# Encoder block on one core: last LayerNorm's rows asked for on SP behind the last weights, joins at the fifth step, one rounding behind LayerNorm

## The chip, the cores and the metric

The kernel runs on one core of a Trainium2 chip. The metric is the device time of one execution in microseconds (us). Engines are named as in the profile: PE is TensorE, DVE VectorE, ACT ScalarE, POOL GpSimd, SP SyncE. SP issues most DMAs, POOL a few.

## The reference

One layer of a streaming encoder on 256 tokens of width 2048, in fp32. Each stage adds to the residual stream and ends in a LayerNorm:

```python
h = layer_norm(ALPHA * h + 0.5 * swiglu_ffn(h, ffn1_w_in[l], ffn1_w_out[l]), ln_ffn1_g[l], ln_ffn1_b[l])
mix = hybrid_mixer(h, w_in[l], gate_bias[l], ...)
h = layer_norm(ALPHA * h + mix, ln_mix_g[l], ln_mix_b[l])
xa = memory_cross_attention(h, mem, ...)
h = layer_norm(ALPHA * h + xa, ln_x_g[l], ln_x_b[l])
h = layer_norm(ALPHA * h + 0.5 * swiglu_ffn(h, ffn2_w_in[l], ffn2_w_out[l]), ln_ffn2_g[l], ln_ffn2_b[l])
```

`swiglu_ffn` is `(silu(x @ w_gate) * (x @ w_up)) @ w_out` with an inner width of 5504, that is 10 groups of 512 columns and one of 384. `layer_norm` ends with `* g + b`; the last one's g and b are rows of `t["gb"]`.

## The kernel before

Weights stream from memory in tiles of 128 x 2048 (1 MB; 128 x 1536 in the 384-column group) through three `raw` buffers. `fetch` (L181 to 186) has SP load one. `halves` (L245) splits it into two fp32r parts: ACT rounds the tile to `hi` (L250), DVE subtracts, `lo = raw - hi` (L253). TensorE multiplies hi by both halves of the activations and lo by the high half. There are two buffers each for `hi` and `lo` (`unit`); weights with named homes (X0, H5 and so on) are rounded into blocks of the activations' pool.

Some steps of a group are done as sums (`mm_sums`, L351): seven products in place of eight for a pair of weight tiles, for which DVE forms sums of the weights (L235, L237), ACT and DVE split those as well (`X` in the 384-column group's rows), and `shared` (L656 to L661) adds up four accumulators afterwards.

The order of work is a list of items. `run` (L172) walks it, and ahead of each item it builds the loads and the splitting of the next weights. Side items are put in by `weave` at given places of a list. A scheduler then orders each engine's instructions by priority and modelled readiness.

`ffn` (L536) runs the two FFNs. For each group of columns it makes the input products (`pair_group`: eight weight steps, of which 2, 4 and 6 are sums, and a `shared` item before the last), then `hidden` (L693): `product` forms silu(gate) * up (L705 to L708) and sorts the 16-bit words (L714), `send` has SP transpose them (L719), `turn` puts the words together again (ACT, L725) and splits them into hi and lo (ACT L242, DVE L243). This last step is called the join here. `send` and `turn` are woven into the next group, at its items 2 and 6; those of the last group, of 384 columns, into the out-projection. TensorE's rows of the 384-column group are L297 and L351 with 128x384; the out-projection follows at once with 128x512.

The last out-projection (`out_proj`, `skewed`) runs its last four weights first for one token half, then for the other, so that the first half's LayerNorm runs beside the second half's matmuls. `final_steps` (L1371) holds that LayerNorm. Its `load` fetches the rows g and b, each spread over the 128 partitions (1 MB each), into the blocks T0 and T1. DVE reads g at L1391 and b at L1395, POOL reads g at L1389.

`mixer` (L834) begins with the value projection `val`, also skewed: the four weights are used for token half 0 and then for token half 1, while the LayerNorm of the first FFN is turned into T (`ln_T`, L390). For each of four quarters `ln_T` normalizes (DVE L397 or ACT L399), transposes (TensorE L405), scales and shifts (ACT L412 and DVE L414 in turn) and splits into T (ACT L242, DVE L243). The third and fourth value weights have homes of their own; the fourth goes to X0 and X1.

Of the kernel before, what the change touches and what calls it, by code (L numbers as in the profile page):

```python
# [18 lines left out]
P = 128  # L19
S = 256  # L20
D = 2048
# [73 lines left out]
class Kernel:  # L95
# [76 lines left out]
    def run(self):  # L172
        queue = [w if isinstance(w, (tuple, Sums)) else (w, None) for _, ws, _, _ in self.items for w in ws]
        ready, nxt, live = [], 0, 0

        def slots(w):
            return 0 if isinstance(w, tuple) and w[1] else 1

        raws, sums = {}, {}

        def fetch(i):  # L181
            if i not in raws:
                ap = queue[i].ap if isinstance(queue[i], Sums) else queue[i][0]
                raws[i] = self.raw_tile()
                self.last_load = self.nc.sync.dma_start(raws[i][:, :ap.shape[1]], ap)
            return raws[i]

        def form_sums(i):
            if i < len(queue) and isinstance(queue[i], Sums) and i not in sums:
                raw, home = fetch(i), queue[i].stage  # L190
                sums[i] = self.weight_sums(raw, queue[i].m, self.block(home, (P, 2048)) if home else self.raw_tile())

        def load(i):
            w = queue[i]
            raw = fetch(i)
            form_sums(i)
            if isinstance(w, Sums):
                n = 4 * w.m
                got = self.halves(raw[:, w.m:n], *self.unit()), self.halves(
                    sums[i][:, :n], *(self.block(g, (P, 2048), F32R) for g in w.tags))  # L200
            else:
                ap, tags = w
                hi, lo = (self.block(g, (P, 2048), F32R) for g in tags[:2]) if tags else self.unit()
                got = self.halves(raw[:, :ap.shape[1]], hi, lo)
            form_sums(i + 1)
            return got

        def early(w):
            return not isinstance(w, Sums) and w[1] is not None and len(w[1]) > 2

        def ahead(need, held):
            if nxt < need:
                return True
            n = sum(not early(w) for w in queue[need:nxt])
            return (nxt < need + 5 and (early(queue[nxt]) or n < 2)
                    and held + live + slots(queue[nxt]) <= UNITS)

        done, highs = 0, []
        for fn, ws, held, prio in self.items:
            need = done + len(ws)  # L220
            while nxt < len(queue) and ahead(need, held):
                live += slots(queue[nxt])
                ready.append(load(nxt))
                highs.append(self.last_hi)
                nxt += 1
            got = [ready.pop(0) for _ in ws]
            live -= sum(slots(queue[done + i]) for i in range(len(ws)))
            done = need
            self.next_hi = highs[min(done, nxt - 1)] if highs else None
            with self.prio(prio):  # L230
                fn(*got)
# [7 lines left out]
        return t  # L239

    def split(self, src, hi, lo):
        self.nc.scalar.copy(hi, src)  # L242
        self.nc.vector.tensor_tensor(lo, src, hi.bitcast(F32), ALU.subtract)  # L243

    def halves(self, src, hi, lo):  # L245

# [143 lines left out]
    def ln_T(self, h, mr, tt, ln, xT, qs=range(4)):  # L390

        nc = self.nc
        mean, r, nb = mr
        for q in qs:
            hs = h[:, q * 512:(q + 1) * 512]
            if q % 2 == 0:
                nc.vector.tensor_scalar(hs, hs, mean, r, ALU.subtract, ALU.mult)  # L397
            else:
                nc.scalar.activation(hs, hs, AF.Identity, bias=nb, scale=r)  # L399
            ps = self.at_tile()  # L400

            with self.tc.issue_after(self.last_mm.ins):
                for j in range(4):
                    kt = 4 * q + j
                    nc.tensor.transpose(ps[:, j * P:(j + 1) * P], h[:, kt * P:(kt + 1) * P], self.ident)  # L405
            v = self.w2((P, 4, P))
            for j in range(4):
                kt = 4 * q + j
                g, b = self.vec(ln + "_g", kt), self.vec(ln + "_b", kt)
                src = ps[:, j * P:(j + 1) * P]  # L410
                if j % 2 == 0:
                    nc.scalar.activation(v[:, j, :], src, AF.Identity, bias=b, scale=g)  # L412
                else:
                    nc.vector.tensor_scalar(v[:, j, :], src, g, b, ALU.mult, ALU.add)  # L414
            hi, lo = (xT.blk(s, 4 * q, 4)[:, :, tt * P:(tt + 1) * P] for s in (0, 1))
            self.split(v, hi, lo)

    def ln_steps(self, ln, st, x):

# [116 lines left out]
    def ffn(self, tag, xT, st, first=None, steps=None, late=None, before=None, tags=None):  # L536
# [6 lines left out]
        for half, nf in enumerate(F_SPLIT):  # L543
            hid, fh, homes = Act([]), {}, SUMS_OUT[half]
            end = half == len(F_SPLIT) - 1
            form = lambda c, fh=fh, homes=homes, hid=hid: self.forms_step(fh, homes, c, lambda: hid)
            for g in range(-(-nf // 4)):
                j, n = f0 // 4 + g, min(4, nf - 4 * g)
                qs, ps = {}, {}
                if j == 2 and first is not None:  # L550
                    self.add(self.load_rest)
                if j == 0 and first is not None:
                    main, (ps, qs, fx) = [], first
                    self.add(lambda qs=qs: self.shared(qs, 512), prio=SOON)
                elif j == 0 and before:
                    main = self.collect(self.first_group, tag, xT, before, ps, fx)
                else:
                    src = t[tag + "_w_in"][j] if n == 4 else t[tag + "_w_in_r"][0]
                    main = self.collect(self.pair_group, bank, src, n * P, KT, xT, SUMS_IN, fx, ps, qs, None, SUM_HOME + ("H5",))
                self.weave(main, turn or {}, prio=0)  # L560
                for c, (home, _) in homes.items():
                    if home == "X1" and c // 2 == g - 1:
                        self.add(form(c))
                hidden, turn = self.hidden(ps, bank, g, n, hid, qs)
                self.add(hidden, prio=SOON)
                if before and 2 <= j < 6:
                    self.add(lambda q=j - 2: self.gb_apply(2, self.h, (q,)), prio=LATE)
                if j == 0 and first is not None:
                    for c in set(SUMS_IN) - set(AT_FIRST):
                        self.add(self.forms_step(fx, SUMS_IN, c, xT, False))  # L570
                bank ^= 1
            if end and late:
                self.add(late)
                self.add(lambda: setattr(self, "cut", True))

            def out(hid=hid):
                x = lambda: hid
                src = [t[tag + "_w_out"][g, :, f0 * 1024:(f0 + nf) * 1024] for g in range(2)]
                self.out_pair(bank, src[0], 0, nf, x, homes, fh, half == 0, st if end else None,
                              SUM_HOME + ("H5",) if end else SUM_HOME)  # L580
                if end:
                    self.out_proj(tag + "_w_out_r", nf, x, False, st, steps, tags, 2, cut=tags is None)
                else:
                    self.out_pair(bank ^ 1, src[1], 1, nf, x, homes, fh, half == 0, None)
            main = self.collect(out)

            side = dict(turn)
            for c, (home, k) in homes.items():
                if home == "X0":
                    side[4 + 2 * k] = side.get(4 + 2 * k, []) + [form(c)]  # L590
            if not end:
                for i in range(2):
                    side[len(main) - 3 + i] = [self.forms_step(fx, SUMS_IN, tuple(SUMS_IN)[i], xT)]
            self.weave(main, side, prio=0)
            turn = None
            f0 += nf
# [237 lines left out]
    def mixer(self, xT, st, steps):  # L834
# [7 lines left out]
        def val(n, tts, g, ps, tags=None, held=0, keep=False, again=False):  # L842
# [17 lines left out]
        ps = {}  # L860
        first = self.collect(lambda: self.skewed(
            lambda tt, g, **kw: val(0, (tt,), g, ps, **kw), (),
            (None, None, ("H5", "H0", "early"), ("X0", "X1"))))
        a, b, c = steps(1)
        self.weave(first, {0: a, 3: b, 4: c})
        gates, fx = {}, {}
# [504 lines left out]
    def final_steps(self, st):  # L1371
# [2 lines left out]

        def load():
            e["gb"] = [self.block(f"T{j}", (P, D)) for j in range(2)]
            for j in range(2):
                nc.gpsimd.dma_start(e["gb"][j], t["gb"][3, j:j + 1, :].to_broadcast([P, D]))

        def steps(tt):  # L1380
            def fn():
# [155 lines left out]
```

## Time and profile before

| what | value |
|---|---|
| median of 3 runs | 2466.49 us (2465.38 to 2469.66) |
| profiled execution | 2466.44 us |
| its span, first to last instruction | 2464.7 us |
| TensorE busy | 2445.8 us, 99% of the span |
| DVE, ACT busy | 2093.3 us (85%), 1447.0 us (59%) |
| DMA | 501.94 MB, mean 204 GB/s |
| mean granted TensorE clock | 0.998 |

Rows of a timeline are: start in us from the span's start, duration in us, engine, line, instruction, what it writes and reads, shape, count, and in brackets how long the engine was idle before it and whom it waited for. `x8` are eight instructions merged; the duration of merged matmuls reaches past the next row's start, since a matmul's end is modelled, so stretches are measured from start to start. SPq and POOLq are the queues of the engines that issue DMAs.

### The profile page before, as it was taken

What the parts mean: (1) busy time and instruction counts of PE and PEld (TensorE: products, weight loads), DVE (VectorE), ACT (ScalarE), POOL (GpSimd) and SP (SyncE); (2) the same over time, 40 slices, a digit from 0 to 9 for tenths busy, and PEclk for the clock granted to TensorE, in tenths of its full rate; (3) what the DMA queues carried; (4) which work ended last, traced back from release to release, by engine and by line L of the source; (5) the groups of instructions that cost most, each with busy time, mean ns of one, the idle gap of its engine ahead of it and who ended that gap; (6) DMA issues with size and microseconds to landing.
All of it is one profiled execution on the core that took longest, in us unless ns stands there. A gap on an engine that the chain in (4) does not pass through costs nothing.

```text
span 2464.7 us, 30068 instructions
## 1 busy us (share of the span) xinstructions
PE 2445.8 (99%) x11603; PEld 2048.8 (83%) x11603; DVE 2093.3 (85%) x2392; ACT 1447.0 (59%) x1932; POOL 37.6 (2%) x81
## 2 busy tenths in 40 slices
PE   9999999999999999999999999999999999999998
PEld 8888888888888888888888888888888888888876
DVE  8999989899778988688788798558879999888886
ACT  6676755676455556556455555545566675557562
POOL 0000000000000001000000000000000000000000
PEclk9999999999999999999999999999999999999999
DMA  7766656666645656554566557544556666666764
GB/s 265 253 217 215 211 203 203 215 197 223 244 156 200 211 205 227 178 174 140 176 235 220 188 179 239 190 161 154 188 197 207 229 221 207 220 213 202 232 210 140
DMA packets 118624, 501.94 MB, mean 204 GB/s; under 512 B 53936, under 2 KB 54704, under 8 KB 63312
## 3 DMA queue, kind: packets, MB, share of 16 engines
q1 hardware_dynamic: 112928, 479.96, 57.4%
q0 software_dynamic: 4688, 18.88, 2.4%
q8 instruction: 91, 1.49, 0.2%
q10 hardware_dynamic: 864, 1.18, 0.1%
q14 instruction: 53, 0.43, 0.1%
HBM read 485.30 MB, written 2.10 MB: 198 GB/s over the span
## 4 chain that ended last, share of the span: by engine, by line
PE 94%; DVE 3%; ACT 1%; DMA 1%; issue 1%; DVEq 0%; SPq 0%; ACTq 0%
PE at L297 24%; PE mm L297 24%; PE at L351 10%; PE mm L351 10%; PE mm L263 9%; PE mm L284 7%; PE mm L265 4%; PE at L986 1%; PE at L284 1%; DVE lo L253 1%; DMA raw<-ffn_w_in_r 1%; PE at L824 1%; PE at L1027 0%; PE at L1346 0%; ACT hi L250 0%
## 5 line engine op out<-in xcount | busy, mean ns | idle before, releaser
L250 ACT CAST hi<-raw 128x1024 fp32r<-128x1024 f32 (+1 forms) x852 | 804.8, 985 | 493.0 <-PE at L297 155.8
L253 DVE TENSOR_TENSOR lo<-raw,hi 128x2048 fp32r<-128x2048 f32 (+1 forms) x427 | 904.7, 2120 | 190.4 <-ACT hi L250 187.7
L297 PE MATMUL mm<-hi,T 128*128 128x512 f32 (+1 forms) x1232 | 288.8, 383 | 0.6 <-ACT hi L250 0.4
L250 ACT CAST X<-H 128x1024 fp32r<-128x1024 f32 (+1 forms) x166 | 170.7, 1034 | 171.3 <-DVE H L235 125.5
L297 PEld LDWEIGHTS mm<-hi,T 128*128 128x128 f32 x1232 | 229.0, 188 | 44.4 <-ACT hi L250 1.1
L297 PE MATMUL at<-hi,T 128*128 128x512 f32 x1072 | 256.7, 389 | 0.0
L253 DVE TENSOR_TENSOR X<-H,X 128x2048 fp32r<-128x2048 f32 (+1 forms) x83 | 186.7, 2250 | 65.0 <-ACT X L250 64.8
L297 PEld LDWEIGHTS at<-hi,T 128*128 128x128 f32 x1072 | 201.1, 188 | 42.0
L297 PE MATMUL mm<-lo,T 128*128 128x512 f32 (+1 forms) x616 | 148.2, 382 | 0.0
L297 PE MATMUL at<-hi,H 128*128 128x512 f32 x592 | 140.8, 390 | 0.0
L297 PE MATMUL at<-lo,T 128*128 128x512 f32 x536 | 132.5, 389 | 0.0
L297 PEld LDWEIGHTS mm<-lo,T 128*128 128x128 f32 x616 | 114.7, 188 | 20.9
L297 PEld LDWEIGHTS at<-hi,H 128*128 128x128 f32 x592 | 110.9, 188 | 23.5 <-DVE w L661 0.6
L263 PE MATMUL mm<-T,hi 128*128 128x512 f32 x512 | 123.7, 393 | 0.0
L297 PEld LDWEIGHTS at<-lo,T 128*128 128x128 f32 x536 | 100.6, 188 | 20.9
L237 DVE TENSOR_TENSOR H<-H,raw 128x512 f32<-128x512 f32 (+1 forms) x166 | 112.3, 676 | 2.3
L263 PEld LDWEIGHTS mm<-T,hi 128*128 128x128 f32 x512 | 93.8, 188 | 19.1 <-issue 0.7
L297 PE MATMUL mm<-hi,H 128*128 128x512 f32 x448 | 108.1, 391 | 0.0
L235 DVE TENSOR_TENSOR H<-raw 128x1024 f32<-128x1024 f32 (+1 forms) x83 | 99.4, 1198 | 4.5 <-DMA raw<-w_gate 4.4
L297 PEld LDWEIGHTS mm<-hi,H 128*128 128x128 f32 x448 | 83.6, 188 | 17.2 <-DVE w L272 0.2
L351 PE MATMUL mm<-X,X 128*128 128x512 f32 x348 | 93.1, 392 | 0.0
L250 ACT CAST X<-raw 128x1024 fp32r<-128x1024 f32 (+1 forms) x54 | 55.3, 1034 | 50.9 <-DVE raw L237 36.9
(331 smaller groups left out, 4074.1 us busy)
## 6 DMA issues: line engine op xcount, KB each, us to landing
raw<-ffn_w_in SPq DMA_DIRECT2D x150, 1024.0 KB, 4.9
raw<-ffn_w_out SPq DMA_DIRECT2D x66, 1024.0 KB, 4.9
raw<-w_gate SPq DMA_DIRECT2D x32, 1024.0 KB, 4.9
raw<-ffn_w_out_r SPq DMA_DIRECT2D x16, 1024.0 KB, 4.9
raw<-w_qk SPq DMA_DIRECT2D x16, 1024.0 KB, 5.0
raw<-w_o_b SPq DMA_DIRECT2D x16, 1024.0 KB, 4.8
raw<-w_out SPq DMA_DIRECT2D x16, 1024.0 KB, 4.9
raw<-w_xk SPq DMA_DIRECT2D x16, 1024.0 KB, 5.1
```

What stands on the lines that cost most here:

```text
L235: self.nc.vector.tensor_tensor(two[0], two[1], raw[:, :m].unsqueeze(1).to_broadcast([P, 2, m]), ALU.add)
L237: self.nc.vector.tensor_tensor(t[:, a * m:a * m + m], t[:, b * m:b * m + m], raw[:, a * m:a * m + m], ALU.add)
L250: self.last_hi = self.nc.scalar.copy(hi[:, c:d], src[:, c:d])
L253: self.nc.vector.tensor_tensor(lo[:, :n], src, hi[:, :n].bitcast(F32), ALU.subtract)
L263: self.nc.tensor.matmul(ps, hi[j], x.both(kt), start=(j == 0), stop=False)
L265: self.last_mm = self.nc.tensor.matmul(ps[:, :S], lo[j], x.at(0, kt), start=False, stop=(j == n - 1))
L284: self.last_mm = self.nc.tensor.matmul(ps, x.at(xi, kt)[:, tt * P:(tt + 1) * P], w[wi][:, j * 512 + c:j * 512 + c + m], start=(start and j ...
L297: self.last_mm = self.nc.tensor.matmul(ps[tt, g][:, :n], x.at(xi, kt)[:, tt * P:(tt + 1) * P], w[wi][:, c:c + n], start=first and j + wi + ...
L351: self.last_mm = self.nc.tensor.matmul(bank[:, :m], a[xi], v[wi][:, c * m:(c + 1) * m], start=own and first and wi + xi == 0, stop=own and ...
L824: self.nc.tensor.transpose(ps[:, i * P:(i + 1) * P], s[:, c:c + P], self.ident)
L986: nc.tensor.matmul(ps[:, c0:c0 + nk], q[:, tt * P:(tt + 1) * P], k[:, :nk], start=(j == 0), stop=(j == len(parts) - 1))
```

## The change

There are three edits.

First, `final_steps.load` issues the two row loads on SP instead of POOL, ordered behind the last weight load that has been built (`last_load`). Its item moves from ahead of the second FFN's last out-projection to six items before that projection's end, where all weight loads have been built.

Second, when the group is the one of 384 columns, the previous group's join is woven in at item 5 instead of 6, in both FFNs.

Third, the fourth value weight of the mixer gets the tag "turned", and its hi and lo are ordered, on ACT, behind the rounding of LayerNorm's second quarter (`ln_act`). The test for early weights looks for the tag's name in place of the number of tags, which finds the same weights as before.

```diff
@@ run / load
-                got = self.halves(raw[:, :ap.shape[1]], hi, lo)
+                with self.tc.issue_after(self.ln_act.ins) if tags and "turned" in tags else nullcontext():
+                    got = self.halves(raw[:, :ap.shape[1]], hi, lo)
@@ run / early
-            return not isinstance(w, Sums) and w[1] is not None and len(w[1]) > 2
+            return not isinstance(w, Sums) and w[1] is not None and "early" in w[1]
@@ split
-        self.nc.scalar.copy(hi, src)
+        copied = self.nc.scalar.copy(hi, src)
         self.nc.vector.tensor_tensor(lo, src, hi.bitcast(F32), ALU.subtract)
+        return copied
@@ ln_T
-            self.split(v, hi, lo)
+            turned = self.split(v, hi, lo)
+            if q == 1:
+                self.ln_act = turned
@@ ffn
+                if turn and n < 4:
+                    turn[5] = turn.pop(6)
                 self.weave(main, turn or {}, prio=0)
@@ ffn
             if end and late:
-                self.add(late)
                 self.add(lambda: setattr(self, "cut", True))
@@ ffn
             side = dict(turn)
+            if end and late:
+                side[len(main) - 6] = [late]
@@ mixer
-            (None, None, ("H5", "H0", "early"), ("X0", "X1"))))
+            (None, None, ("H5", "H0", "early"), ("X0", "X1", "turned"))))
@@ final_steps
-            for j in range(2):
-                nc.gpsimd.dma_start(e["gb"][j], t["gb"][3, j:j + 1, :].to_broadcast([P, D]))
+            with self.tc.issue_after(self.last_load.ins):
+                for j in range(2):
+                    nc.sync.dma_start(e["gb"][j], t["gb"][3, j:j + 1, :].to_broadcast([P, D]))
```

The line numbers of the changed kernel are higher by up to 8. On SP, at the end of the program, the order before was the last weights (`raw`) and then the output:

```order
L185 DMA raw_19153<-ffn_w_out_r 128x2048
L185 DMA raw_19160<-ffn_w_out_r 128x2048
L185 DMA raw_19179<-ffn_w_out_r 128x1536
L1396 DMA out<-h_101 128x512 x2
L1396 DMA out<-h_102 128x512 x2
```

Now the same place on SP holds the two rows of gb (T_2962 is the scale, T_2963 the offset), which POOL no longer issues:

```order
L185 DMA raw_19156<-ffn_w_out_r 128x2048
L185 DMA raw_19175<-ffn_w_out_r 128x1536
L1386 DMA T_2962_19206<-gb 128x2048
L1386 DMA T_2963_19207<-gb 128x2048
L1404 DMA out<-h_101 128x512 x2
```

They stand behind the last weight and ahead of the output.

On ACT, in the second half of the 384-column group of the first FFN, before the change (`hi_4294` is step 5's weight, `X_644` and `X_653` are the weight sums of steps 4 and 6, L725 and `H_658` the join, L656 and L657 are `shared`):

```order
L250 CAST hi_4294<-raw_4292 128x512
L250 CAST X_644_4263<-H_637_4227 128x1024
L250 CAST hi_4326<-raw_4299 128x1024
L250 CAST X_644_4263<-H_637_4227 128x512
L250 CAST hi_4326<-raw_4299 128x128
L250 CAST hi_4362<-raw_4360 128x1024
L250 CAST hi_4362<-raw_4360 128x512
L250 CAST X_653_4331<-H_650_4301 128x1024
L656 COPY w_662_4402<-at_4233 128x384
L250 CAST X_653_4331<-H_650_4301 128x512
L725 COPY w_614_4090<-w_615_4091 128x2x512
L725 COPY w_616_4092<-w_617_4093 128x2x512
```

And after the change, from the same cast on:

```order
L252 CAST hi_4294<-raw_4292 128x512
L732 COPY w_614_4090<-w_615_4091 128x2x512
L252 CAST X_644_4263<-H_637_4227 128x1024
L243 CAST H_655_4336<-w_614_4090 128x4x128
L252 CAST hi_4326<-raw_4299 128x1024
L252 CAST X_644_4263<-H_637_4227 128x512
L252 CAST hi_4326<-raw_4299 128x128
L732 COPY w_616_4092<-w_617_4093 128x2x512
L243 CAST H_655_4336<-w_616_4092 128x4x128
L252 CAST hi_4369<-raw_4367 128x1024
L252 CAST hi_4369<-raw_4367 128x512
L252 CAST X_653_4331<-H_650_4301 128x1024
```

One join now stands ahead of X_644's first cast and the other ahead of step 7's weight. On TensorE four matmuls of step 5 stand ahead of the first that reads X_644, where one stood. On DVE, at the end of the same group, the order before was (`lo_4398` is the low half of the first out-weight; L658 to L661 `shared`, L705 and L706 the product, and two rows of the join, L243):

```order
L243 TENSOR_TENSOR H_658_4367<-w_614_4090,H_658_4367 128x4x128
L658 TENSOR_TENSOR w_664_4404<-w_662_4402,at_4235 128x384
L243 TENSOR_TENSOR H_658_4367<-w_616_4092,H_658_4367 128x4x128
L659 TENSOR_TENSOR w_663_4403<-w_663_4403,w_664_4404 128x384
L706 TENSOR_TENSOR w_662_4402<-w_662_4402,mm_4156 128x384
L660 TENSOR_TENSOR w_664_4404<-w_664_4404,at_4236 128x384
L661 TENSOR_TENSOR w_665_4405<-w_663_4403,at_4236 128x384
L706 TENSOR_TENSOR w_664_4404<-w_664_4404,mm_4158 128x384
L705 TENSOR_TENSOR w_663_4403<-w_663_4403,mm_4157 128x384
L705 TENSOR_TENSOR w_665_4405<-w_665_4405,mm_4159 128x384
L253 TENSOR_TENSOR lo_4398<-raw_4395,hi_4397 128x2048
```

Now it is:

```order
L255 TENSOR_TENSOR lo_4398<-raw_4395,hi_4397 128x2048
L665 TENSOR_TENSOR w_664_4404<-w_662_4402,at_4235 128x384
L666 TENSOR_TENSOR w_663_4403<-w_663_4403,w_664_4404 128x384
L713 TENSOR_TENSOR w_662_4402<-w_662_4402,mm_4156 128x384
L667 TENSOR_TENSOR w_664_4404<-w_664_4404,at_4236 128x384
L668 TENSOR_TENSOR w_665_4405<-w_663_4403,at_4236 128x384
```

The low half moved ahead of all these, and the join's subtractions to earlier in the group. The second FFN has the same rows under other numbers.

On ACT, where the mixer starts, before (`X_786` is the fourth value weight; L412 with `w_773` to `w_779` are the pieces of LayerNorm's quarters 0 to 3; `T_768` and `T_769` the first two quarters' roundings):

```order
L399 ACTIVATE h_101<-h_101,nb_5094,y_5091 128x512 x2
L250 CAST X_786_5226<-raw_5224 128x1024
L412 ACTIVATE w_773_5151<-at_5146,vecs 128x128
L250 CAST X_786_5226<-raw_5224 128x1024
L412 ACTIVATE w_773_5151<-at_5146,vecs 128x128
L412 ACTIVATE w_775_5164<-at_5159,vecs 128x128
L242 CAST T_768_5141<-w_773_5151 128x4x128
```

After the change:

```order
L401 ACTIVATE h_101<-h_101,nb_5094,y_5091 128x512 x2
L414 ACTIVATE w_773_5151<-at_5146,vecs 128x128
L414 ACTIVATE w_775_5164<-at_5159,vecs 128x128
L414 ACTIVATE w_773_5151<-at_5146,vecs 128x128
L414 ACTIVATE w_775_5164<-at_5159,vecs 128x128
L243 CAST T_768_5141<-w_773_5151 128x4x128
L243 CAST T_769_5142<-w_775_5164 128x4x128
L252 CAST X_786_5226<-raw_5224 128x1024
```

Both casts of X_786 stand behind the two roundings now.

## Prediction

> **What bounds the kernel now.** I read the page first (engines, then the chain that ended last), then TensorE's waits, then the timelines of the engines around each wait.
>
> ```profile
> PE 2445.8 (99%) x11603; PEld 2048.8 (83%) x11603; DVE 2093.3 (85%) x2392; ACT 1447.0 (59%) x1932; POOL 37.6 (2%) x81
> ...
> PE 94%; DVE 3%; ACT 1%; DMA 1%; issue 1%; DVEq 0%; SPq 0%; ACTq 0%
> ```
>
> TensorE (PE) works 2445.8 of 2464.7 us and holds 94% of the chain. The edits change none of its matmuls, so only its stalls can be won. Its waits name them:
>
> ```profile
> PE at L351 <- ACT X L250: 2.1, 3, 1.0
> PE at L297 <- DVE lo L253: 2.0, 2, 1.0
> ...
> PE mm L284 <- DVE T L243: 0.4, 1, 0.4
> PE mm L284 <- ACT T L242: 0.3, 1, 0.3
> ```
>
> The columns are the total, the count and the longest in us. The first row lies in the 384-column group of the second FFN, the second behind that group in both FFNs, and the last two where the mixer starts. These are the three places of the change.
>
> **Part one: scale and offset behind the last weights.** The 384-column group runs twice with the same instructions, once per FFN, but only in the second do the two gb loads fall into it. TensorE's timeline (start, duration, instruction, count, idle before):
>
> ```profile
> 547.79 2.96 PE L297 MATMUL mm<-hi,T 128*128 128x384 f32 x16
> ...
> 551.98 2.93 PE L297 MATMUL mm<-hi,T 128*128 128x384 f32 x16
> ...
> 565.62 0.34 PE L297 MATMUL mm<-hi,T 128*128 128x384 f32 x1
> ...
> 572.38 0.51 PE L351 MATMUL mm<-hi,T 128*128 128x384 f32 x2
> ...
> 580.44 3.97 PE L297 MATMUL at<-hi,H 128*128 128x512 f32 x16
> 585.43 2.11 PE L297 MATMUL at<-lo,H 128*128 128x512 f32 x8 [1.03 <-DVE lo L253]
> ```
>
> ```profile
> 2313.69 2.96 PE L297 MATMUL mm<-hi,T 128*128 128x384 f32 x16
> ...
> 2349.55 4.02 PE L297 MATMUL at<-hi,H 128*128 128x512 f32 x16
> 2354.57 2.11 PE L297 MATMUL at<-lo,H 128*128 128x512 f32 x8 [0.99 <-DVE lo L253]
> 2356.51 3.79 PE L297 MATMUL at<-hi,H 128*128 128x512 f32 x16
> 2360.14 1.98 PE L297 MATMUL at<-lo,H 128*128 128x512 f32 x8
> ```
>
> From the group's first matmul to the same low-half matmul the first FFN takes 585.43 - 547.79 = 37.64 us, the second 2354.57 - 2313.69 = 40.88. The **3.24 us** between them are what the loads cost, if they are the cause. The DMA issues in the two stretches (550 to 575, then 2316 to 2343), with the median time to landing:
>
> ```profile
> raw<-ffn_w_in_r SPq DMA_DIRECT2D x4, 768.0 KB, 4.5
> ```
>
> ```profile
> raw<-ffn_w_in_r SPq DMA_DIRECT2D x4, 768.0 KB, 6.4
> T<-gb POOLq DMA_DIRECT2D x2, 1024.0 KB, 6.7
> ```
>
> The same four weight tiles take 1.9 us longer each beside the two gb loads, and the chain there runs through them. Moved away, they leave the first FFN's timing: I take 3.24; the bounds are 0 (the weights are late for another cause) and 3.24.
>
> Where they go, behind the last weight on SP, must be free too. The last weight's issue, its landing, and who reads it and the two rows:
>
> ```profile
> 2430.43 0.33 SPq L185 DMA_DIRECT2D raw<-ffn_w_out_r  x1
> ```
>
> ```profile
> raw<-ffn_w_out_r SPq DMA_DIRECT2D x1, 768.0 KB, 4.2
> ```
>
> ```profile
> 2436.20 3.95 DVE L253 TENSOR_TENSOR X<-raw,X 128x2048 fp32r<-128x2048 f32 x2
> ...
> 2444.24 0.74 DVE L1391 SCALAR_TENSOR_TENSOR h<-h,mv,T 128x512 f32<-128x512 f32 x1
> ...
> 2448.63 2.73 DVE L1395 SCALAR_TENSOR_TENSOR h<-h,y,T 128x512 f32<-128x512 f32 x4
> ```
>
> The scale would be issued near 2430.8. If it lands one 6.7 behind the weight's own landing at 2434.6, that is 2441.3, 2.9 us before L1391 reads it; the offset another 6.7 later, 2448.0, still before L1395. These are contended times, one after the other, so a pessimistic case. SP's later work, the output's DMAs, waits for L1395 in any case. I cost the new place at nothing. The trace has no broadcast on SP; the nearest row for a slow one is
>
> ```profile
> X<-gate_row POOLq DMA_DIRECT2D x4, 512.0 KB, 6.2
> ```
>
> and at its rate 1 MB takes 12.4 us: that is the upper bound, used in the last rival.
>
> **Part two: joins one step earlier.** Sixteen full-width matmuls normally take 2360.14 - 2356.51 = 3.63 us before the low half starts. Behind the 384-column group it is 585.43 - 580.44 = 4.99 and 2354.57 - 2349.55 = 5.02: 1.36 + 1.39 = **2.75 us** lost, waiting for VectorE's low half of the first out-weights, which stands behind the joins' two subtractions, the sums and the hidden product:
>
> ```profile
> 582.17 1.01 DVE L705 TENSOR_TENSOR w<-w,mm 128x384 f32<-128x384 f32 x2
> 583.10 2.28 DVE L253 TENSOR_TENSOR lo<-raw,hi 128x2048 fp32r<-128x2048 f32 x1
> ```
>
> In the changed order ten operations of VectorE no longer stand ahead of that low half: two subtractions of the joins, four of the sums, four of the product. At 0.5 each (the first row has two in 1.01) it starts near 578.1 and ends near 580.4, and TensorE asks for it at 580.44 + 3.63 = 584.07. What becomes late instead: the sums (L660, L661) free the fourth accumulator up to 2.28 us later, and the changed order puts that accumulator's matmuls last. So I count the 2.75 whole.
>
> The price is paid in step 5. There ScalarE now makes one join copy before it rounds the sums' weights X:
>
> ```profile
> 538.91 1.35 ACT L725 COPY w<-w 128x1024 uint16<-128x1024 uint16 x1
> ...
> 562.87 1.57 ACT L250 CAST hi<-raw 128x1024 fp32r<-128x1024 f32 x2 [3.17 <-PE mm L297]
> ```
>
> The casts end at 564.44, the copy at 565.79, and X's first cast (about 1.05) at 566.84. TensorE now has four matmuls ahead of it instead of one, at (551.98 - 547.79) / 24 = 0.175 us each, so it comes at 565.62 + 0.70 = 566.32 and **waits 0.5**. But this step already loses as much: its 36 matmuls should take 6.30 us and take 572.38 - 565.62 = 6.76. After X's first part the changed order has work enough for the rest of X. I take the net at 0; the bounds per group are +0.46 (old wait gone, none new) and -2 (a whole join, 1.35 and about 0.6 of rounding, shows). The second join fits into ScalarE's idle time before step 7.
>
> On SP one out-weight load now goes ahead of the two transposes of the 384-column hidden block. Those are read by
>
> ```profile
> 608.80 2.00 ACT L725 COPY w<-w 128x768 uint16<-128x768 uint16 x2
> ```
>
> more than 20 us after the out steps begin at 580.44: nothing.
>
> **Part three: one rounding behind LayerNorm.** The mixer's first matmuls need LayerNorm's first two quarters; on ScalarE two casts of the fourth value weight (X, which TensorE reads only in the fourth value step) stand between their pieces. ScalarE's, TensorE's and VectorE's rows:
>
> ```profile
> 697.09 1.14 ACT L242 CAST T<-w 128x512 fp32r<-128x512 f32 x2
> ```
>
> ```profile
> 681.22 1.04 PE L405 MATMUL at<-ident,h 128*128 128x128 f32 x8
> ...
> 684.18 1.04 PE L405 MATMUL at<-ident,h 128*128 128x128 f32 x8
> 685.55 0.50 PE L284 MATMUL mm<-hi,T 128*128 128x512 f32 x1 [0.34 <-ACT T L242]
> ...
> 689.10 2.00 PE L284 MATMUL mm<-hi,T 128*128 128x512 f32 x8
> ...
> 694.58 1.04 PE L405 MATMUL at<-ident,h 128*128 128x128 f32 x8
> 695.37 2.98 PE L284 MATMUL mm<-X,T 128*128 128x512 f32 x12
> ```
>
> ```profile
> 697.74 1.29 DVE L243 TENSOR_TENSOR T<-w,T 128x512 fp32r<-128x512 f32 x2 [0.25 <-ACT T L242]
> ```
>
> Eight transposes take 695.37 - 694.58 = 0.79, so the twelve matmuls could run from 684.97 and need 12 x 0.227 = 2.72, to 687.69. They end at 689.10: **1.41 us** lost. The second token half shows the chain without casts between: transposes at 694.58, T rounded by 697.66 (+3.1), low half by 698.4 (+3.8). From the first half's transposes at 681.22 that gives 684.3 and 685.0: just in time. Behind the casts that now wait stand the third and fourth quarters' pieces, some 2 us later; TensorE reads those two steps of 2.72 after 684.97, at 690.4. VectorE's low half of X keeps its place behind the second half's scaling. That half's own chain then has little room, for which I take off 0.15: 1.25, between 0 and 1.41.
>
> **Sum.** 3.24 + 2.75 + 0 + 1.25 = 7.24. The profiled execution took 2466.44 us (span 2464.7 and 1.74 around it); the median of the runs is 2466.49, so one number serves for both: 2466.44 - 7.24 = **2459.2**.
>
> **The rivals.**
> - *The joins' wait only moves.* ScalarE, first in first out, shows a join before X in each group. At the bound of -2 twice, less the 2.75, part two is -1.25 and the time 2463.2; half of it gives 2461.2. For it: X is just in time already. Against: four matmuls moved ahead of it.
> - *The weights of the second group are late for another cause.* Then part one is worth nothing and the time is 2462.4. Against: 4.5 against 6.4 in the two landing rows.
> - *The last weight is slowed by the row loads behind it.* If it lands like the contended ones (6.4, not 4.2), VectorE's last low half moves from 2440.15 to 2442.35. TensorE asks for it 18 matmuls after the row below starts, at 2441.5: 0.8 lost, 2460.0. For it: on another queue these loads did slow the weights. Against: here they are issued only behind the weight.
>
> ```profile
> 2437.45 4.93 PE L284 MATMUL mm<-X,H 128*128 128x512 f32 x21
> ```
>
> The Trainium skill (DMA: Bandwidth & Descriptors, "Two DMAs through the same engine are not ordered") says that descriptors of one queue start in order, but that a later one may finish before an earlier one has written. By that the weight could be late as in this rival, and by plain order in the queue it would land in 4.2 as before; no run here shows it yet.
> - *The rows land late: slower.* At gate_row's rate, one after the other behind the weight, the offset lands at 2434.6 + 24.8 = 2459.4, 10.8 after L1395 wants it; 10.8 - 7.24 gives 2470.0. It costs from a landing after 2448.6, and the kernel is slower than before once that is 7.2 later. Against: the gb rows took 6.7 each with weights beside them, on the other queue.
>
> **How the numbers follow.** Forecast 0.62 (own range 2457.8 to 2461.5), joins 0.16, other cause 0.08, last weight 0.08, late rows 0.04, anything else 0.02. The low end, 2457.4, is every bound at its best (3.24 + 2.75 + 0.92 + 1.41 = 8.3, and a little for the scatter of runs); the high end, 2463.6, takes in the first two rivals. Within 0.2% (about what a measurement of this kernel can tell from no change) means above 2461.6. Faster 0.71, same 0.24, slower 0.05.
>
> **What would show it.** In the new profile the two low-half waits behind the 384-column groups are gone; the second group's weights land in 4.5 again and it takes as long as the first; TensorE runs through the mixer's first twelve matmuls in under 3 us; a new wait of about half a us for X stands in step 5 of both groups. The forecast is wrong if X's wait is over 1 us, if L1391 or L1395 waits for a DMA, or if the stalls come back as waits further on.

## The result and the profile after

| kernel | median, us | runs | ratio to the kernel before |
|---|---|---|---|
| before | 2467.88 (2465.38 to 2469.66) | 7 | |
| after | 2458.82 (2458.64 to 2460.78) | 7 | 0.9967 [0.9957, 0.9977] |

The change gains 0.33%, 8.1 us by the ratio. The forecast was 2459.2, a gain of 7.24. The first profiled execution of the changed kernel is the slowest of its seven, 2460.78 us with a span of 2459.0; a second one, told below, has 2457.5. The page of the first, engines and then chain:

```profile
PE 2443.1 (99%) x11603; PEld 2048.7 (83%) x11603; DVE 2093.3 (85%) x2392; ACT 1447.9 (59%) x1932; POOL 36.6 (1%) x79
...
PE 98%; DVE 1%; ACT 0%; issue 0%; DMA 0%; DVEq 0%; SPq 0%; ACTq 0%
```

TensorE runs the same 11603 matmuls; its share of the chain rose from 94% to 98%, because waits went. TensorE's waits in that execution (total, count, longest):

```profile
PE at L407 <- issue: 1.9, 1, 1.9
PE at L479 <- DVE w L456: 1.1, 1, 1.1
PE at L353 <- ACT X L252: 0.4, 2, 0.2
```

The waits for X (2.1 in three) and for the low half (2.0 in two) of before are gone, but for two of 0.2. The second row stood before too, at the kernel's start. The first row, 1.9 at the transposes of LayerNorm, is new ("issue" means that the profile shows nothing that was waited for); the experiments come to it. TensorE's timelines of the two 384-column groups, first FFN, then second:

```profile
565.40 0.86 PE L299 MATMUL mm<-hi,T 128*128 128x384 f32 x4
566.44 0.98 PE L353 MATMUL at<-X,X 128*128 128x384 f32 x4 [0.19 <-ACT X L252]
...
580.17 2.92 PE L299 MATMUL at<-hi,H 128*128 128x512 f32 x12
...
585.65 3.79 PE L299 MATMUL at<-hi,H 128*128 128x512 f32 x16
```

```profile
2312.80 2.96 PE L299 MATMUL mm<-hi,T 128*128 128x384 f32 x16
...
2331.68 0.97 PE L353 MATMUL at<-X,X 128*128 128x384 f32 x4 [0.19 <-ACT X L252]
...
2345.39 2.92 PE L299 MATMUL at<-hi,H 128*128 128x512 f32 x12
...
2350.87 3.79 PE L299 MATMUL at<-hi,H 128*128 128x512 f32 x16
```

The second group's out step starts 2345.39 - 2312.80 = 32.59 us after the group, 35.86 before; the step lasts 2350.87 - 2345.39 = 5.48 with no wait in it, 6.96 before. The low half that TensorE used to wait for, on VectorE, and the weights of the second group (issues from 2312 to 2340, median time to landing last):

```profile
578.17 2.28 DVE L255 TENSOR_TENSOR lo<-raw,hi 128x2048 fp32r<-128x2048 f32 x1
```

```profile
raw<-ffn_w_in_r SPq DMA_DIRECT2D x5, 768.0 KB, 4.3
```

It starts at 578.17 where 583.10 was, and the weights land in 4.3, where 6.4 were, with no gb beside them. The rows and the last weight at their new place (issues from 2420 to 2440; SP's timeline; VectorE's readers):

```profile
T<-gb SPq DMA_DIRECT2D x2, 1024.0 KB, 7.8
...
raw<-ffn_w_out_r SPq DMA_DIRECT2D x1, 768.0 KB, 4.7
```

```profile
2425.16 0.90 SPq L1386 DMA_DIRECT2D T<-gb  x2
```

```profile
2438.74 0.74 DVE L1399 SCALAR_TENSOR_TENSOR h<-h,mv,T 128x512 f32<-128x512 f32 x1
...
2443.13 2.73 DVE L1403 SCALAR_TENSOR_TENSOR h<-h,y,T 128x512 f32<-128x512 f32 x4
```

The two rows land 6.8 and 8.8 us behind their issues (7.8 is the median of the two), by 2434.4 at the latest, and are read from 2438.7 and 2443.1 on: both readers carry no bracket, so nothing waits.

All that follows is read at three places. From the first matmul of each 384-column group: to the start of the out step, and to that of the next step behind it (24 matmuls on). At the mixer: from the transposes of LayerNorm's third and fourth quarters to the end of the first twelve matmuls. In us, from TensorE's timelines of one profile each:

| kernel | first FFN's group | second FFN's group | mixer | span |
|---|---|---|---|---|
| before | 32.65 / 39.59 | 35.86 / 42.82 | 4.92 | 2464.7 |
| after | 32.60 / 38.08 | 32.59 / 38.07 | 3.81 | 2459.0 |
| e1_rows | 32.60 / 39.55 | 32.37 / 39.36 | 5.27 | 2461.6 |
| e2_joins | 32.64 / 38.12 | 36.02 / 41.50 | 4.37 | 2461.5 |
| e3_round | 32.62 / 39.58 | 35.24 / 42.19 | 3.66 | 2462.7 |
| e4_rows_sp_old | 32.48 / 39.42 | 33.10 / 40.54 | 5.29 | 2464.6 |
| e5_rows_pool_late | 32.42 / 39.39 | 36.15 / 43.10 | 4.44 | 2464.3 |
| e6_joins4 | 32.51 / 37.99 | 32.63 / 38.11 | 3.63 | 2457.1 |
| e7_after_again | 32.62 / 38.10 | 32.61 / 38.09 | 3.60 | 2457.5 |
| e8_join_behind_x | 32.44 / 37.92 | 32.43 / 37.91 | 3.63 | 2457.1 |
| e9_after_sp_old | 32.65 / 38.14 | 33.69 / 39.17 | 3.62 | 2458.5 |
| e10_one_row | 32.64 / 38.12 | 33.96 / 39.44 | 3.80 | 2459.0 |
| e11_after_pool_old | 32.70 / 38.18 | 34.14 / 39.62 | 3.67 | 2461.1 |

### The profile page after: what moved, and what is told of

It reads as the page before. It is cut to its first block, busy times and chain, and to the rows that moved or that the text cites. A ratio compares the mean times of both kernels' runs of the same rounds, so it can differ in the third digit from the quotient of the medians.

```text
span 2459.0 us, 30064 instructions
## 1 busy us (share of the span) xinstructions
PE 2443.1 (99%) x11603; PEld 2048.7 (83%) x11603; DVE 2093.3 (85%) x2392; ACT 1447.9 (59%) x1932; POOL 36.6 (1%) x79
## 3 DMA queue, kind: packets, MB, share of 16 engines
q8 instruction: 91, 1.49, 0.2%
## 4 chain that ended last, share of the span: by engine, by line
PE 98%; DVE 1%; ACT 0%; issue 0%; DMA 0%; DVEq 0%; SPq 0%; ACTq 0%
PE mm L299 25%; PE at L299 25%; PE at L353 11%; PE mm L353 11%; PE mm L286 9%; PE mm L265 9%; PE mm L267 4%; PE at L993 1%; PE at L286 1%; PE at L831 1%; PE at L1034 0%; PE at L1353 0%; PE at L1329 0%; PE at L407 0%; DVE h L1403 0%; PE at L1035 0%
```

## The experiments

### Each part alone

The theory is the prediction's: three stalls, each undone by its own edit. The rivals are that the joins' wait only moves, and that the second group is late for another reason.

**e1_rows**: the kernel before, with the first edit only.

```diff
-                self.add(late)
+                side[len(main) - 6] = [late]
...
-                nc.gpsimd.dma_start(e["gb"][j], t["gb"][3, j:j + 1, :].to_broadcast([P, D]))
+            with self.tc.issue_after(self.last_load.ins):
...
+                    nc.sync.dma_start(e["gb"][j], t["gb"][3, j:j + 1, :].to_broadcast([P, D]))
```

> Only the two row loads are moved (SP, behind the last weight); joins and the mixer's rounding stay as before. Theory (the loads took bandwidth from the second 384-column group's weights): the second group takes 37.6 us from its first matmul to the first low half of the out-projection, like the first group (before 40.9), the four 768 KB weights land in 4.3 to 5.0 us (before 6.4), the low-half wait of 1.0 us behind both groups stays, and the time falls by 3.2 us. Rival one (those weights are late for another cause): the group stays at 40.9 and the time within 1 us. Rival two (the last weight or the rows come late at the end): the last weight lands over 6 us after its issue, or VectorE waits for a DMA in the last LayerNorm, and part of the 3.2 is lost there.

Measured 2463.47 us (2462.73 to 2466.74) against 2466.9, ratio 0.9988 [0.9980, 0.9997]. TensorE's second group:

```profile
2314.15 2.96 PE L297 MATMUL mm<-hi,T 128*128 128x384 f32 x16
...
2346.52 3.98 PE L297 MATMUL at<-hi,H 128*128 128x512 f32 x16
2351.53 2.14 PE L297 MATMUL at<-lo,H 128*128 128x512 f32 x8 [1.03 <-DVE lo L253]
2353.51 3.80 PE L297 MATMUL at<-hi,H 128*128 128x512 f32 x16
```

It falls to the first's times, 39.36 against 39.55, and the low-half wait stays in both. The rows beside its weights were the cause of all the 3.2 us between the groups.

**e2_joins**: the kernel before, with the second edit only.

```diff
+                if turn and n < 4:
+                    turn[5] = turn.pop(6)
```

> Only the joins are moved to the fifth step of the 384-column group. Theory (VectorE's queue ahead of the out-projection's first low half cost TensorE 1.4 to 1.5 us in each FFN): from the group's first matmul to the second out step the first FFN takes 38.1 us (before 39.6), the low-half waits are gone, a wait of 0.2 us for X stands in step 5, and the time falls by 2.9 us; the second group keeps the 3.2 us of the row loads. Rival (the wait only moves): X's wait in step 5 is 1 us or more per group, or the low-half wait is still there, and the time stays within 1 us.

Measured 2462.9 us (2460.23 to 2466.04), ratio 0.9984 [0.9975, 0.9993]. Both out steps are 5.48 long: the low-half waits go without the rows' help. In the first group the join's price in step 5 is a wait of 0.20 and the group's time to the out step is as before (32.64). In the second, still beside the rows, TensorE waits 1.69 for X.

**e3_round**: the kernel before, with the third edit only.

```diff
+                with self.tc.issue_after(self.ln_act.ins) if tags and "turned" in tags else nullcontext():
```

> Only the fourth value weight's rounding is ordered behind LayerNorm's second quarter. Theory (two casts in ScalarE's queue held back the first quarters): from the transposes of quarters 2 and 3 to the end of the mixer's first twelve matmuls 3.8 us (before 4.9), later steps as before, the time falls by 1.1 us. Rival (the chain from statistics to transposes sets it, not the casts): it stays at 4.9, or the 1.1 us come back as waits for the third quarter or for X within the next 20 us; the time stays within 0.3 us.

Measured 2465.7 us (2462.61 to 2467.7), ratio 0.9991 [0.9982, 0.9999]. TensorE at the mixer:

```profile
684.21 1.04 PE L407 MATMUL at<-ident,h 128*128 128x128 f32 x8
...
687.87 1.98 PE L286 MATMUL mm<-hi,T 128*128 128x512 f32 x8
```

The mixer's place falls from 4.92 to 3.66, no later step of it waits, and the groups keep their stalls. The place varies from execution to execution, but the two sets don't meet: 4.37 to 5.29 in the five profiles without this edit, 3.60 to 3.81 in the eight with it.

By their ratios the three are worth 3.0, 3.9 and 2.2 us, 9.1 in all beside 8.1 for the change, each uncertain by about 2. That can't tell whether the parts add up. Read at the places they are worth 3.46, 1.47 + 1.32 and 1.26, 7.5 in all, as much as the changed kernel gains there (told below), though e2's second group has a stretch at half clock in it.

### Place in the program, queue and number of rows

**e4_rows_sp_old**: the kernel before, with the rows issued by SP at their old place.

```diff
-                nc.gpsimd.dma_start(e["gb"][j], t["gb"][3, j:j + 1, :].to_broadcast([P, D]))
+                nc.sync.dma_start(e["gb"][j], t["gb"][3, j:j + 1, :].to_broadcast([P, D]))
```

> The kernel before with the two row loads on SP in place of POOL, at their old place in the program. Theory (what costs is 2 MB moved beside the weights, whatever queue): the second 384-column group takes 40.9 us or up to 5 more, since on SP the rows stand ahead of weights; the time is the same as before or up to 5 us more. Rival (POOL's queue is what slows the weights): the group falls to 37.6 and the time by 3.2 us, as with the loads moved.

Measured 2465.1 us (2464.17 to 2466.9), ratio 0.9994 [0.9985, 1.0003]. To the low-half matmul the second group takes 38.59: neither the 40.88 of before nor the 37.64 without rows beside it. This missed, and e9 and e11 were made to see why.

**e5_rows_pool_late**: the kernel before, with the rows built at the new place but on POOL and with no order.

```diff
-                self.add(late)
+                side[len(main) - 6] = [late]
```

> The kernel before with the two row loads built six items before the end of the last out-projection, but still issued by POOL and with no order behind the last weight. Theory: on POOL nothing stands in front of them, so they are issued as soon as T0 and T1 are free, where they were before (2322.5 and 2330.4 in the profile before); the second 384-column group still takes 35.9 us to its first out step and 42.8 to the second, its weights land in about 6.2, and the time is that of the kernel before. Rival: the place in the program decides when they are issued; then the group takes 32.4 and 39.4 as with the rows on SP behind the last weight, and the time falls by 3.0 to 3.4.

Measured 2466.48 us (2464.97 to 2468.23), ratio 0.9998 [0.9990, 1.0007]; the group takes 43.10. Later in the program alone does nothing: POOL has nothing in front of these loads.

**e9_after_sp_old** and **e11_after_pool_old**: the changed kernel, with the rows back at their old place, on SP and on POOL, both without the order. **e10_one_row**: the scale's row alone back on POOL.

```diff
+                self.add(late)
-                side[len(main) - 6] = [late]
-            with self.tc.issue_after(self.last_load.ins):
```

> The changed kernel with the two row loads back at their old place in the program, but issued by SP and without the order behind the last weight. From the run with the rows on SP at the old place of the kernel before (40.5 us to the second out step, where 39.4 is without rows beside the weights and 42.8 with them on POOL), theory: in one queue with the weights they cost about 1.1 us, so the second group takes about 39.2 and the time is 1 above the changed kernel's. Rival: that run was a chance, and the 2 MB cost the same on either queue, 3.4: the group takes 41.5 and the time is 3 above.

> The changed kernel with both row loads back on POOL at their old place, so the joins and the rounding without the rows. Theory: the parts add up: the second group takes 41.5 us to the second out step, as with the joins alone, the mixer's first twelve matmuls end 3.6 us after the transposes' start, and the time is 3.2 to 3.4 above the changed kernel's, near 2462.3. Rival: the parts overlap, and with both other stalls gone the rows' lateness finds cover: less than 2 above.

> The changed kernel with the scale's row alone back on POOL at its old place; the offset's row stays on SP behind the last weight. Theory: each row delays the weights that land beside it, so one of two costs about half of 3.4, 1.7: the second group takes 39.8 us to the second out step and the time is 1.7 above the changed kernel's. Rival: the group has slack for one row (its weights wait up to a us or two in raw before they are rounded), and only two together show: 38.1 and no difference.

Measured on one chip beside 2466.2 for the kernel before: e9 2460.57 us (ratio 0.9977 [0.9967, 0.9986]), e10 2461.64 (0.9983 [0.9974, 0.9993]), e11 2461.58 (0.9979 [0.9970, 0.9988]).

*In the changed kernel one row costs about as much as two.* The group takes 39.44 with one and 39.62 with two, where 38.09 is without: 1.35 and 1.53. The expected half fell, and so did its rival that one row is covered. In both profiles the group has a single wait of over 0.2, for X in step 5 (1.56 and 1.70); behind the second row's landing there is none. The delayed weight shows why: ScalarE begins to round it 16.48 us into the group with one row and 16.64 with two (15.08 in e7, without rows). The second row is issued only 16.7 us into the group (2330.0 in e11), when that weight has just landed.

*Queue or order?* In e9 the group loses 1.08, as expected from e4. But ScalarE's order differs. Its rows in e11, then in e9:

```profile
2329.94 1.57 ACT L252 CAST hi<-raw 128x1024 fp32r<-128x1024 f32 x2 [4.73 <-DMA raw<-ffn_w_in_r]
2331.42 1.34 ACT L731 COPY w<-w 128x1024 uint16<-128x1024 uint16 x1
2332.63 1.03 ACT L252 CAST X<-H 128x1024 fp32r<-128x1024 f32 x1
```

```profile
2327.80 1.57 ACT L252 CAST hi<-raw 128x1024 fp32r<-128x1024 f32 x2 [4.71 <-DMA raw<-ffn_w_in_r]
2329.27 1.57 ACT L252 CAST X<-H 128x1024 fp32r<-128x1024 f32 x2
```

Counted from each group's start (2313.30 and 2311.17) the delayed weight is rounded at the same point, 16.64 and 16.63, so SP's queue did not bring it sooner. In e9 X follows at once, while in e11 the join copy is between: moving the loads to another engine made the scheduler order ScalarE another way. In e4 it moved too: four matmuls of step 5 stand ahead of X on TensorE there, where the kernel before has one, and the delayed weight is rounded from 16.84 on, hardly sooner than the 17.11 of before. So these two runs don't show that the queue matters; with one profile each they don't exclude it either.

*Is the rows' price fixed?* Beside the joins at step 5 it was 1.53 in e11's profile, which its rival had (under 2), but 41.50 - 38.09 = 3.41 in e2's, which the theory had. e11's time, 2.5 us above e7's below (3.0 by the ratios, uncertain by some 2), lies between. Its profile has one more stall, which isn't the rows': a wait of 1.88 at another LayerNorm's transposes, at 1764. TensorE's rows behind its wait for X, in e2 and in e11:

```profile
2332.67 1.34 PE L351 MATMUL at<-X,X 128*128 128x384 f32 x4 [1.69 <-ACT X L250]
2333.80 2.76 PE L297 MATMUL mm<-hi,T 128*128 128x384 f32 x8
2336.36 0.56 PE L351 MATMUL at<-X,X 128*128 128x384 f32 x2
```

```profile
2333.71 0.96 PE L353 MATMUL at<-X,X 128*128 128x384 f32 x4 [1.70 <-ACT X L252]
2334.51 1.57 PE L299 MATMUL mm<-hi,T 128*128 128x384 f32 x8
2335.92 0.51 PE L353 MATMUL at<-X,X 128*128 128x384 f32 x2
```

The wait is the same. But then the same eight matmuls take 2336.36 - 2333.80 = 2.56 us in e2 and 2335.92 - 2334.51 = 1.41 in e11. The table by stage of e2 has the granted clock in the third column from the right:

```profile
2330.00:2332.60 2.60, 0.97 (x4) 0.65 (x4) 2.10 (x2) 2.60 (x4) 0.00 (x0) 1.00 0.96 352
2332.60:2336.40 3.80, 3.73 (x13) 3.73 (x14) 2.59 (x4) 3.77 (x7) 0.00 (x0) 0.56 0.88 281
2336.40:2340.00 3.60, 3.60 (x22) 3.60 (x21) 3.20 (x4) 0.57 (x2) 0.00 (x0) 0.99 0.71 291
```

After the wait TensorE ran at half clock for 3.4 us (with rows of a tenth of a us: 2333.05 to 2336.46), half of which is 1.7; from X to the out step e2 takes 15.24 us and e11 13.73, so 1.5 of it reached the group. e5's profile has the same at 2334.7 to 2338.1, behind waits of 0.89 and 1.02. The profile before has waits of 1.02 and 0.85 in that group, without it. So a wait of 1 to 2 us costs itself, and in two of these profiles nearly as much again. The landing differs as well: the delayed weight is rounded 16.6 us into the group in e11, 17.0 in e2, 17.1 before and 17.8 in e5, whose edit leaves the rows where they were before.

### The late transposes

**e7_after_again**: the changed kernel, no edit.

> The changed kernel once more, without an edit. In its first profile the transposes that turn LayerNorm's third and fourth quarter for the mixer start at 684.55, though the first FFN's 384-column group had ended 1.5 us sooner than before; behind 684.18 - 1.5 that is 1.9 us late. Theory: the value weights landed late in that one execution by chance (ScalarE waited 3.5 and 2.8 us for w_va there, 1.0 and 1.6 in the profile before); then this profile has these transposes near 682.6 and a span near 2457. Rival: the change itself delays those weights, with 684.5 and a span of 2459 again.

Measured 2459.12 us (2458.65 to 2459.74), ratio 0.9967 [0.9955, 0.9979], span 2457.5. The mixer's start on TensorE, in the first profile of the changed kernel and in this one:

```profile
681.57 1.06 PE L407 MATMUL at<-ident,h 128*128 128x128 f32 x8 [1.92 <-issue]
```

```profile
683.13 1.04 PE L407 MATMUL at<-ident,h 128*128 128x128 f32 x8
683.92 2.06 PE L286 MATMUL mm<-hi,T 128*128 128x512 f32 x8
685.82 1.07 PE L286 MATMUL mm<-lo,T 128*128 128x512 f32 x4
686.73 1.98 PE L286 MATMUL mm<-hi,T 128*128 128x512 f32 x8
```

The wait of 1.92 isn't there, and the twelve matmuls run from 683.92 to 686.73, in 2.81. The value weights (issues from 645 to 668) landed in 7.7 in the first profile and in 5.6 here and before:

```profile
raw<-w_va SPq DMA_DIRECT2D x3, 1024.0 KB, 7.7
```

```profile
raw<-w_va SPq DMA_DIRECT2D x3, 1024.0 KB, 5.6
```

So that loss is of one execution, not of the change: in e6 and in e8 to e11 too the first transposes start 131.8 to 132.0 us behind the first group, as in e7 (131.95), and only in the first profile 134.0. The kernel before is not free of it: e4 has a wait of 0.81 at the same place. Why the weights were late stays open.

### The wait that is left

**e6_joins4**: the changed kernel with the join at item 4. **e8_join_behind_x**: the changed kernel with the join copies ordered behind X's first cast.

```diff
-                    turn[5] = turn.pop(6)
+                    turn[4] = turn.pop(6)
```

```diff
-                with self.tc.issue_after(self.next_hi.ins):
+                with self.tc.issue_after((self.first_sums[-2] if late_join else self.next_hi).ins):
```

> The changed kernel with the join at item 4 instead of 5 of the 384-column group. In its order both join copies stand on ScalarE behind X's casts of the sums' step, and the next sums' X is asked for earlier on TensorE. Theory: the wait for X in step 5 comes from the one join copy ahead of X's first cast (0.35 us by starts, 0.19 shown in brackets), so it goes in both groups, and the groups take about 32.25 to the out step and 37.7 to the second; the time is 0.7 under the changed kernel's, too little to measure. Rival: two copies back to back (2 x 1.36) on ScalarE come ahead of the following weight's rounding, and TensorE waits 1 to 2 us there; then the groups take 33.5 to 34.5 and the time is 2 to 4 us above the changed kernel's.

> The changed kernel, with the join copies of the 384-column group ordered behind X's first cast on ScalarE; on TensorE one matmul of step 5 stands ahead of X again, where four stood. Theory: X's cast now starts where the copy started (564.1 in the changed kernel's profile) and ends near 565.2, before TensorE asks for it at 565.6, so the wait for X goes from both groups; they take 32.25 to the out step and 37.7 to the second, and the two joins, 1.0 us later, are still done before VectorE comes to the first out-weight's low half. Time 0.7 under the changed kernel's, hardly to be measured. Rival: X's sums, not the copy, are what its cast waits for; then the wait of 0.2 to 0.5 stays. Third: the later joins push the low half of the first out-weight back, and the wait of about 1 us behind the group returns.

Measured, beside e7's 2459.12: e6 2458.91 us (2458.84 to 2459.02), ratio 0.9969 [0.9956, 0.9981]; e8 2459.13 (2458.73 to 2461.49), 0.9971 [0.9960, 0.9983]. In both the wait for X in step 5 is gone, so the copy ahead of X was its cause. In e8 both groups are 0.18 shorter, the wait's length, not the 0.35 expected: X's cast now waits for VectorE's sums,

```profile
564.93 1.06 ACT L253 CAST X<-H 128x1024 fp32r<-128x1024 f32 x1 [0.29 <-DVE H L239]
566.04 0.97 PE L356 MATMUL at<-X,X 128*128 128x384 f32 x4
```

and ends at 565.99, just as TensorE asks (ScalarE's row, then TensorE's). In e6 the first group gains 0.11 and the second nothing. The rivals' waits, of 1 to 2 us in e6 and of about 1 behind e8's groups, didn't come. Neither of the two beats the changed kernel by an amount that the times can tell.

## Why the prediction was right, point by point

The second profile of the changed kernel, undisturbed at the mixer, against the profile before:

| term | predicted | measured |
|---|---|---|
| first group: joins | 1.36 | 39.59 - 38.10 = 1.49 |
| second group: rows and joins | 3.24 + 1.39 = 4.63 | 42.82 - 38.09 = 4.73 |
| rounding behind LayerNorm | 1.25 | 4.92 - 3.60 = 1.32 |
| sum | 7.24 | 7.54 |
| span | | 2464.7 - 2457.5 = 7.2 |

The rest is the kernel's start, 0.44 longer in that execution (the first group starts at 548.23 instead of 547.79, behind three waits of 0.2 to 0.5 in the first 9 us), and 0.1 between the places. That the median of 2458.82 lies within 0.4 of the forecast is partly luck: the forecast was counted from one execution of the kernel before, 2466.44, and the same 7.24 off the median of the seven, 2467.88, would be 2460.6.

- **The rows.** Taking the same group in the first FFN for the group without the rows held: e1's second group is within 0.2 of its first, and the rows alone are worth 42.82 - 39.36 = 3.46 there (3.24, which the step took for its upper bound). What the step did not see is that this price is no constant: with both rows on POOL it was 1.5 to 3.7 in single profiles, by when the delayed weight landed, by ScalarE's order and by the clock.
- **The new place.** Right at no cost. From the second group's next step to the end of the span e7 takes 107.98 us, where 108.19 were. The rival of the slowed last weight is seen in small: it lands in 4.7 (4.2 before, 6.4 feared), which TensorE doesn't notice; it is 4.7 to 4.8 in all six profiles with a row behind the weight, 4.2 to 4.5 in the seven without. The Trainium skill (DMA: Bandwidth & Descriptors, "Two DMAs through the same engine are not ordered") has descriptors of one queue of an engine start in order, while a later one may finish before an earlier one has written; the traces show 0.2 to 0.6 us for this weight. The rows, issued 0.4 apart, landed 6.8 and 8.8 behind their issues, so side by side; one after the other at 12.4 each is out.
- **The joins.** The low half was forecast to start near 578.1 and end near 580.4: it started at 578.17 and ended at 580.45. The net of nothing in step 5 held too: from 565.40 to 572.12 its 36 matmuls take 6.72, where 6.76 were. The new wait for X was forecast at 0.5; by starts it is 566.44 - 565.40 - 0.70 = 0.34, and taking it away (e8) is worth 0.18.
- **The rounding.** 1.32 in e7 and 1.26 in e3, against 1.25, though the 4.92 it is counted from was 4.37 to 5.29 in single profiles; the 0.15 kept back for the second half wasn't needed, as its transposes and twelve matmuls run without a bracket.
- **The rivals.** "The joins' wait only moves" fell in e2's first group and in both groups of e7, where the wait is 0.2. "Late for another cause" fell in e1. "Late rows" fell in the profile after.

## What to carry to other kernels

Where a kernel runs the same code twice, the undisturbed run is the price list for the disturbed one: the difference of two stretches gave the rows' cost within 0.3 us. A load that is needed only at the end is worth moving behind the last load of its queue, but its place in the program alone needn't do that: built later on an idle engine's queue it was issued at the same moment as ever, 8.8 us into the group (e5). The order behind the last weight was run only together with the move to SP (e1); SP without it at the new place was not. And when an edit moves the time, look at how it moved the other engines' instructions before a queue gets the credit (e9).

## What the runs showed of the hardware

A wait of 1.69 us on TensorE was followed by half clock for 3.4 us in e2, and two waits of 0.89 and 1.02 close together were in e5. Five waits of 1.56 to 1.92 in other profiles were not: one each in the first profile of the changed kernel, e4 and e10, and two in e11, one of them 1.70 at the very place of e2's. The Trainium skill (TensorE: Matmul & The Clock Gate, "Part 1: The HAM clock gate (the "warmup" mystery)") has half the clock after an idle window of about 3.4 us, and the full clock after a busy window of the same length. The slow stretches here agree with the second, 3.4 us; the idle time ahead of them, 1.7 and 1.9, was about half of the first. What decides between the two outcomes stays open. Small waits thus have two prices, and one profile shows one of them.
